# A relative-bias table stored once instead of in 128 copies: a two-layer decoder trunk on one core

## The chip, the cores and the metric

The kernel runs on one core of a Trainium2 chip. The metric is the device time of one execution in microseconds (us). The core has five engines that run side by side and meet through semaphores: TensorE (PE; the profile lists its weight loads apart as PEld), VectorE (DVE), ScalarE (ACT), GpSimd (POOL) and SyncE (SP). Sixteen DMA engines move data between DRAM and the core's memory. A DMA is issued by one of the engines; those of SyncE, ScalarE and GpSimd go through queues of their own to the same sixteen DMA engines.

## The reference, cut to what matters

A sequence of 256 tokens of width 2048 passes two layers, each with a residual, and a last norm. Layer 0 is a gated linear recurrence, layer 1 a sparse attention with three branches (compressed, selected, window) of 16 heads in 4 groups. To the logits of all three branches a relative bias is added, which depends only on the head and on the distance between query and key, through 32 buckets.

```python
def t5_bucket(dist):
    n = jnp.maximum(dist, 0)
...
    return jnp.where(n < max_exact, n, large)
...
    tab = rel_bias.astype(jnp.float32).reshape(NUM_BUCKETS, G, hpg).transpose(1, 0, 2)
...
        logit_c = jnp.einsum('bgqhd,bgkd->bgqhk', qb, K_cmp) + bias_shared(dist_c)
        p_c = masked_softmax(logit_c, (dist_c >= 0)[:, None, :])
...
        logit_s = jnp.einsum('bgqhd,bgqkd->bgqhk', qb, k_g) + bias_s
...
        logit_w = jnp.einsum('bgqhd,bgkd->bgqhk', qb, k_wb) + bias_shared(dist_w)
```

So one table of 16 heads x 256 distances, with a mask value for keys after the query, serves every query: row t of a head's bias is the table, shifted by t.

## The kernel before, in words

**The stream of weights.** All weights are float32 and are read once, in pieces of 128 x 1024 (512 KB). SyncE issues the load of a piece into a `raw` buffer (`emit_load`, L120). ScalarE rounds it to a high part `hi` (L132), VectorE subtracts to get the low part `lo` (L142), and TensorE multiplies in three products: high with high, high with low, low with high (`mm3`, L150). A `plan` lists the pieces in order. Six `raw` buffers and four pairs of split buffers let loads run up to eight pieces and splits up to four pieces ahead of the products; a buffer is loaded again when VectorE has made the low part out of it.

**The other work** is written as generators, which take a step before and a step after the products of each piece (`run`, `advance`). This fixes each engine's order of instructions in the program; the engines then run through their own orders as far as semaphores let them.

**Layer 0** makes four passes (s = 0 to 3), each over four chunks of 512 columns: `f`, `q`, `v`, `z`. Once the `q` chunk is multiplied, VectorE scales it into `QQ` (L439), multiplies by the gate (L457), and TensorE starts the products of the scores (L472), which come behind the first piece of the `v` chunk. Once `v` is multiplied, ScalarE evacuates it (L445).

**The bias table.** `setup` makes it at the start: GpSimd fills `bk` with the bucket number of every distance (L351), by falling distance, VectorE compares to get one-hot columns, one product with the 32 x 16 parameter gives 16 x 256 values, and VectorE copies them into `brev` (L383), 16 rows of 384; the last 128 columns hold the mask value (L352). `store_bias` writes it to DRAM: four DMAs issued by GpSimd (L405), one per four heads, each writing every row 128 times, so that the DRAM tensor `brev_dram` has a copy for each of the 128 partitions. It is started with a delay of eight pieces after layer 0's first `f` chunk, and its steps put four turns between the DMAs.

**The skewed reads.** For each group of four heads in layer 1, `get_bias` issues two DMAs on GpSimd (L836), each for two heads: partition p reads 256 values of its own copy, from column 127 - p. So partition p holds the bias of query p (and of query 128 + p, with other columns), key by key. Group 0's are issued after the window values' projection, those of the next group at the tenth turn of `attend`, when VectorE has done its last head; two buffers.

**Attention.** `attend` runs a head in three slots: TensorE's logits, VectorE's sums with the bias with a running maximum, six per head (`biased`, L871: 128, 7, 128, 256, 15 and 256 keys), ScalarE's exponentials (L878), the weighing by VectorE (L889) and ScalarE (L887), TensorE's transposes (L898). The 7 and the 15 compressed keys read the bias at every 16th column. Slices of the tile `bi` at L860 to L865 pick the columns:

```python
            bi = bias[h // 2][:, h % 2]
...
                   (0, b0[:, 0:7], bi[:, 159:256:16], l[:, 256:263]),
...
                   (4, b1[:, 0:256], bi, l[:, 304:560]),
```

Of the kernel before, what the change touches and what calls it, by code (L numbers as in the profile page):

```python
# [45 lines left out]
def kernel(ctx: ExitStack, tc: tile.TileContext, x, norm_gains, final_gain, rel_bias,  # L46
# [40 lines left out]
        nc.vector.tensor_copy(dst, tp[:, :S])  # L87
        nc.vector.tensor_scalar(scaled, tp[:, :S], QSCALE, None, op0=ALU.mult)

    # ---- the stream of weights: pieces are loaded ahead, split exactly into two parts that one-pass  # L90
    # float32 products carry, and multiplied; between pieces, steps of the other work run ----
    plan = []
    loaded, parts = {}, {}
    steps = []
# [101 lines left out]
            if j == 0 and between:  # L196
                between()

    # Each slot multiplies one piece. A step of other work takes a turn before the products (work that
    # depends on earlier slots) and one after them (products, and what may wait), in turn.  # L200
    def run(gen, delay=0):
        def late():
            for _ in range(2 * delay):
# [62 lines left out]
            advance()  # L266

    x1_dram = dram.tile([S, D], F32, name="x1_dram")
    brev_dram = dram.tile([P, NH, 384], F32, name="brev_dram")

    ctxs = {n: ExitStack() for n in ("xg", "start")}
    xgp = ctxs["xg"].enter_context(tc.tile_pool(name="xgp", bufs=1))
# [17 lines left out]
    pair = lambda ap: ap.rearrange("p (a t) -> p a t", a=2)  # L290
    hgain = pcol[:, 0, 48:49]

# [1 line left out]
    sp = ctxs["start"].enter_context(tc.tile_pool(name="start", bufs=1))  # L294
    xt = sp.tile([P, 2, D], F32, name="xt")
    ssqp = sp.tile([P, 2, 4], F32, name="ssqp")
# [34 lines left out]
        rstd_of(rstd0, ssq, D)  # L331

    prow = sp.tile([P, 2, P], F32, name="prow")
    brev = const.tile([NH, 384], F32, name="brev")
    rb = sp.tile([BUCKETS, NH], F32, name="rb")

    def setup():
        # masks of the levels inside a 32 x 32 block: the highest bit in which t and s differ, s < t
        si = sp.tile([P, 32], I32, name="si")
        ti = sp.tile([P, 32], I32, name="ti")  # L340
        nc.gpsimd.iota(si, pattern=[[0, 32]], base=0, channel_multiplier=1)
        nc.gpsimd.iota(ti, pattern=[[1, 32]], base=0, channel_multiplier=0)
        pidx = sp.tile([P, 1], F32, name="pidx")
        nc.gpsimd.iota(pidx, pattern=[[0, 1]], base=0, channel_multiplier=1, allow_small_or_imprecise_dtypes=True)
        thr = sp.tile([P, 7, 32], F32, name="thr")
        for l in range(7):
            nc.gpsimd.memset(thr[:, l], float(2 ** l // 2))
        bk = sp.tile([BUCKETS, 256], F32, name="bk")
        for b in range(BUCKETS):
            n0, n1 = T5_LO[b], (T5_LO[b + 1] if b + 1 < BUCKETS else 256)  # L350
            nc.gpsimd.memset(bk[:, 256 - n1:256 - n0], float(b))  # L351
        nc.gpsimd.memset(brev[:, 256:], NEG)  # L352
        for _ in range(6):
            yield
        nc.vector.tensor_scalar(si, si, 31, None, op0=ALU.bitwise_and)
        xi = sp.tile([P, 32], I32, name="xi")
        nc.vector.tensor_tensor(xi, si, ti, op=ALU.bitwise_xor)
        nc.vector.tensor_scalar(rowmask, pidx, float(CMP_BLOCK - 1), None, op0=ALU.is_ge)
        oneh = sp.tile([BUCKETS, 256], F32, name="oneh")
        nc.vector.tensor_scalar(oneh, bk, pidx[:BUCKETS], None, op0=ALU.is_equal)  # L360
        gt = sp.tile([P, 32], F32, name="gt")
        nc.vector.tensor_tensor(gt, ti, si, op=ALU.is_ge)
        xf = sp.tile([P, 32], F32, name="xf")
        nc.gpsimd.tensor_copy(xf, xi)
        yield
        yield
        cg = sp.tile([P, 7, 32], F32, name="cg")
        nc.vector.tensor_tensor(cg, xf[:, None, :].to_broadcast([P, 7, 32]), thr, op=ALU.is_ge)
        nc.vector.tensor_mul(cg, cg, gt[:, None, :].to_broadcast([P, 7, 32]))
        mf = sp.tile([P, 6, 32], F32, name="mf")  # L370
        nc.vector.tensor_sub(mf, cg[:, 0:6], cg[:, 1:7])
        nc.gpsimd.tensor_copy(masks, mf)
        yield
        yield
        yield
        pp = aux_bank()
        for i in range(2):
            nc.tensor.transpose(pp[:, i * P:(i + 1) * P], prow[:, i, :], ident)
        nc.tensor.matmul(pp[:NH, 256:512], rb, oneh, start=True, stop=True)
        yield  # L380
        nc.vector.tensor_copy(pcol.rearrange("p a b -> p (a b)"), pp[:, :2 * P])
        # relative bias by reversed distance, masked keys at NEG; one row per partition for skewed reads
        nc.vector.tensor_copy(brev[:, :256], pp[:NH, 256:512])  # L383
        yield
        # lower bounds: softmax over the depth rows, cumulated up to row 0
        lb3 = pcol[:, 0, 0:48].rearrange("p (a h) -> p a h", a=3)
        lbm = sp.tile([P, NH], F32, name="lbm")
        lbe = sp.tile([P, 3, NH], F32, name="lbe")
        nc.vector.tensor_max(lbm, lb3[:, 0], lb3[:, 1])
        nc.vector.tensor_max(lbm, lbm, lb3[:, 2])  # L390
        nc.vector.tensor_sub(lbe, lb3, lbm[:, None, :].to_broadcast([P, 3, NH]))
        yield
        nc.scalar.activation(lbe, lbe, AF.Exp)
        lbs = sp.tile([P, NH], F32, name="lbs")
        yield
        nc.vector.tensor_add(lbs, lbe[:, 0], lbe[:, 1])
        nc.vector.tensor_add(lbs, lbs, lbe[:, 2])
        nc.vector.reciprocal(lbs, lbs)
        nc.vector.tensor_mul(lb, lbe[:, 0], lbs)
        nc.vector.tensor_scalar(oml, lb, -1.0, 1.0, op0=ALU.mult, op1=ALU.add)  # L400

    def store_bias():
        for i in range(4):
            hs = slice(4 * i, 4 * i + 4)
            nc.gpsimd.dma_start(brev_dram[:, hs].rearrange("p h j -> h p j"),  # L405
                                brev[hs, None, :].to_broadcast([4, P, 384]))
            for _ in range(4):
                yield

# [1 line left out]
    HG = {}  # L411

    def f_of(s, ps):
# [182 lines left out]
        add_chunk(w_in1, 4096 + 512 * s, 512, "n", X, v_done)  # L596
        add_chunk(w_in1, 6144 + 512 * s, 512, "n", X, on_z)

# [1 line left out]
    ssq1 = const.tile([P, 2, 4], F32, name="ssq1")  # L600
    ssum = const.tile([P, 2], F32, name="ssum")
    tok = lambda ap, c0, n: ap[:, c0:c0 + n].rearrange("(t p) c -> p t c", p=P)
# [59 lines left out]
        add_chunk(w_out1, 512 * c, 512, "n", (yh, yl), on_x1(c),  # L662
                  extra={1: [residual(("x", c - 1), x_rows, 512 * (c - 1), 512)]} if c else None)

# [1 line left out]
    NS = {}  # L666

    def open_ns():
# [14 lines left out]
        NS["hid"], NS["gelu"] = (scratch[:, c0:c0 + 64].rearrange("p (g n) -> p g n", g=G) for c0 in (512, 576))  # L683
        NS["bia"] = scratch[:, 640:641]
        nc.gpsimd.memset(NS["hid"][:, :, NCMP:], 0.0)
        # three products of the two parts in one: high, low and high parts below each other
        for name, shape in (("Vc", [P, 512]), ("pc", [P, 2, 2, P])):
            NS[name] = n1.tile(shape, F32R, name=name)
            nc.gpsimd.memset(NS[name].bitcast(F32), 0.0)
# [142 lines left out]

    def get_bias(g, a):
        b = NS["p2"].tile([P, 2, S], F32, tag="bias", name="bias", bufs=BIAS_BUFS)
        src = brev_dram[:, 4 * g + 2 * a:4 * g + 2 * a + 2, :]
        nc.gpsimd.dma_start(b, bass.AP(tensor=src.tensor, offset=src.offset + HD - 1,  # L836
                                       ap=[[NH * 384 - 1, P], [384, 2], [1, S]]))
        NS["bias"][a] = b

    def attend(g):  # L840
# [3 lines left out]
        pT, L = {}, {}  # L844

        def logits(h):
            # keys of a group: the first compressed 8 again, selected 256, compressed 16, window 256
            b0, b1, b2 = aux_bank(), aux_bank(), aux_bank()
            ks = [t[:, g] for t in NS["K"]]
            first = [bass.AP(tensor=k.tensor, offset=k.offset, ap=[list(k.ap[0]), [280, 2], [1, 136]]) for k in ks]  # L850
            for tt, dst, (kh, kl) in ((0, b0[:, 0:272], first), (1, b1[:, 0:272], [k[:, 8:280] for k in ks]),
                                      (1, b2[:, 0:256], [k[:, 280:536] for k in ks])):
                qh, ql = (t[:, h % 2, tt * P:(tt + 1) * P] for t in NS["q", g, h // 2])
                mm3(dst, qh, ql, kh, kl, True, True)
            l = ns.tile([P, 816], F32, tag="L", name="L", bufs=1)
            mx = ns.tile([P, 6], F32, tag="mx", name="mx")
            sm = ns.tile([P, 6], F32, tag="sm", name="sm")
            bi = bias[h // 2][:, h % 2]
            nc.gpsimd.memset(l[:, 263:288], 0.0)
            prt = ((1, b0[:, 8:136], bi[:, 128:256], l[:, 0:128]),  # L860
                   (0, b0[:, 0:7], bi[:, 159:256:16], l[:, 256:263]),
                   (2, b0[:, 136:264], bi[:, 128:256], l[:, 128:256]),
                   (4, b1[:, 0:256], bi, l[:, 304:560]),
                   (3, b1[:, 256:271], bi[:, 31:256:16], l[:, 288:303]),
                   (5, b2[:, 0:256], bi, l[:, 560:816]))  # L865
            L[h] = l, sm, prt, mx
# [104 lines left out]
    def gated(g, ps, ov):  # L971
# [6 lines left out]
        for a in range(2):  # L978
            nc.scalar.activation(zs[a], zs[a], AF.Silu)
        if g + 1 < G:  # L980
            # the exponential's table is loaded back ahead of its use
            nc.scalar.activation(NS["one"], NS["one"], AF.Exp, scale=0.0)
        steps_between = (3, 2, 5) if g + 1 < G else (1, 2, 2)
        for _ in range(steps_between[0]):
# [39 lines left out]
        else:  # L1024
            add_chunk(w_in2, C_Z + 512 * g, 512, "t", X, z_done1(g))

# [1 line left out]
    FN = {}  # L1028

    def open_fin():  # L1030
# [113 lines left out]
```

## Time and profile before

| What | Value |
|---|---|
| Median of three runs | 1010.38 us (1009.32 to 1012.52) |
| Span of the profiled execution | 1007.5 us |
| Mean granted clock of TensorE | 0.990 |
| DMA packets, bytes | 105405, 182.28 MB |
| Read from DRAM, written to DRAM | 173.62 MB, 7.34 MB |

The profiled execution's span, from its first to its last instruction, is 1007.5 us; the runs' times hold a little more than a span, and the median stands 2.9 us above it. In the profile a row of the page's slices is the span cut into 40 pieces of 25.2 us, each digit the busy share in tenths. A group row has the line, the engine, the operation, what is written from what, a count, and then busy time and the mean length of one. A row of waits names who waited for whom, the total, how often, and the longest. DMA rows give the size of one transfer and the median time from its issue to its landing.

### The profile page before, as it was taken

The page shows a single profiled execution, that of the slowest core. Times are in us where ns is not written, and L with a number is a line of the kernel's source. Part 1 is how long each engine was busy: PE and PEld are TensorE (multiplying, and loading weights), DVE is VectorE, ACT ScalarE, POOL GpSimd, SP SyncE. Part 2 cuts the span into 40 slices and gives each one's busy share as a digit, 9 for nine tenths or more (in the row PEclk, how much of TensorE's full clock was granted, in tenths as well). Part 3 has the DMA queues.
Part 4 walks back from the last instruction along what each step waited for, and adds up shares of the span by engine and source line. Part 5 has one row for each costly group of instructions (what it writes and reads, how often), then busy time and mean ns, then how long its engine had stood idle before and what let it go on. Part 6 is the DMA issues. An engine that isn't in the chain of part 4 may idle for free.

```text
span 1007.5 us, 19899 instructions
## 1 busy us (share of the span) xinstructions
PE 979.9 (97%) x8001; PEld 906.5 (90%) x8001; DVE 630.1 (63%) x1194; ACT 519.4 (52%) x896; POOL 55.0 (5%) x157
## 2 busy tenths in 40 slices
PE   8949999999999999999999999999999999999997
PEld 7947899789978997888889999899999999998887
DVE  6718555855586558655556565555677787776564
ACT  6603455245524552454444554443766877875442
POOL 2200100010001000100002000000000000000000
PEclk9978999999999999999999999999999999999999
DMA  9797656465646454647677776566454545456662
GB/s 325 151 137 221 197 154 189 130 198 153 188 129 202 151 189 128 202 158 234 218 233 237 226 217 190 154 208 189 147 148 131 166 137 155 129 166 230 208 215 99
DMA packets 105405, 182.28 MB, mean 181 GB/s; under 512 B 8128, under 2 KB 27152, under 8 KB 105184
## 3 DMA queue, kind: packets, MB, share of 16 engines
q1 hardware_dynamic: 100512, 171.86, 54.4%
q0 software_dynamic: 4464, 8.61, 4.7%
q8 instruction: 63, 1.03, 0.4%
q10 hardware_dynamic: 336, 0.54, 0.1%
q14 instruction: 30, 0.25, 0.1%
HBM read 173.62 MB, written 7.34 MB: 180 GB/s over the span
## 4 chain that ended last, share of the span: by engine, by line
PE 93%; DMA 4%; ACT 1%; DVE 1%; issue 1%; SPq 0%; POOLq 0%; POOL 0%; DVEq 0%; ACTq 0%
PE mainps L150 82%; PE auxps L150 5%; DMA raw<-in_hgrn_w_in_dram 3%; PE auxps L472 2%; DMA xt<-in_x_dram 1%; PE auxps L898 1%; PE auxps L483 0%; PE auxps L531 0%; PE auxps L529 0%; PE auxps L530 0%; PE auxps L487 0%; PE auxps L554 0%; PE auxps L629 0%; PE auxps L900 0%; ACT hi L132 0%
## 5 line engine op out<-in xcount | busy, mean ns | idle before, releaser
L142 DVE TENSOR_TENSOR lo<-raw,hi 128x1024 fp32r<-128x1024 f32 (+3 forms) x317 | 380.6, 1208 | 198.1 <-ACT hi L132 197.2
L132 ACT CAST hi<-raw 128x1024 fp32r<-128x1024 f32 (+3 forms) x317 | 328.5, 1038 | 340.8 <-PE mainps L150 293.9
L150 PE MATMUL mainps<-xh,hi 128*128 128x256 f32 x1280 | 365.4, 286 | 0.0
L150 PE MATMUL mainps<-xh,lo 128*128 128x256 f32 x1280 | 362.1, 283 | 0.0
L150 PE MATMUL mainps<-xl,hi 128*128 128x256 f32 x1280 | 362.0, 283 | 0.0
L150 PEld LDWEIGHTS mainps<-xh,hi 128*128 128x128 f32 x1280 | 244.8, 191 | 0.8 <-ACT hi L132 0.4
L150 PEld LDWEIGHTS mainps<-xl,hi 128*128 128x128 f32 x1280 | 244.9, 191 | 0.2
L150 PEld LDWEIGHTS mainps<-xh,lo 128*128 128x128 f32 x1280 | 244.7, 191 | 0.0
L150 PE MATMUL mainps<-hi,xh 128*128 128x512 f32 (+1 forms) x352 | 135.1, 384 | 0.0
L150 PE MATMUL mainps<-lo,xh 128*128 128x512 f32 (+1 forms) x352 | 131.5, 374 | 0.0
L150 PE MATMUL mainps<-hi,xl 128*128 128x512 f32 (+1 forms) x352 | 131.2, 373 | 0.0
L150 PE MATMUL mainps<-hi,yh 128*128 128x512 f32 (+1 forms) x288 | 105.9, 368 | 0.0
L150 PE MATMUL mainps<-hi,yl 128*128 128x512 f32 (+1 forms) x288 | 105.3, 366 | 0.0
L150 PE MATMUL mainps<-lo,yh 128*128 128x512 f32 (+1 forms) x288 | 105.3, 366 | 0.0
L150 PEld LDWEIGHTS mainps<-hi,xl 128*128 128x128 f32 x352 | 66.5, 189 | 11.7
L150 PEld LDWEIGHTS mainps<-hi,xh 128*128 128x128 f32 x352 | 66.5, 189 | 11.7 <-issue 0.2
L150 PEld LDWEIGHTS mainps<-lo,xh 128*128 128x128 f32 x352 | 66.6, 189 | 10.2
L150 PEld LDWEIGHTS mainps<-hi,yl 128*128 128x128 f32 x288 | 54.3, 189 | 8.8
L150 PEld LDWEIGHTS mainps<-hi,yh 128*128 128x128 f32 x288 | 54.4, 189 | 8.5
L150 PEld LDWEIGHTS mainps<-lo,yh 128*128 128x128 f32 x288 | 54.4, 189 | 8.5
L878 ACT ACTIVATE L<-L,mx 128x128 f32<-128x128 f32 (+1 forms) x96 | 37.6, 393 | 24.3 <-DVE mx L873 24.2
L472 PEld LDWEIGHTS auxps<-QQ,Kg 128*32 128x32 f32 x1280 | 15.0, 113 | 21.7 <-DVE QQ L457 14.9
(241 smaller groups left out, 868.9 us busy)
## 6 DMA issues: line engine op xcount, KB each, us to landing
raw<-in_hgrn_w_in_dram SPq DMA_DIRECT2D x127, 512.0 KB, 3.7
raw<-in_nsa_w_in_dram SPq DMA_DIRECT2D x104, 512.0 KB, 3.9
raw<-in_hgrn_w_out_dram SPq DMA_DIRECT2D x32, 512.0 KB, 5.0
raw<-in_nsa_w_out_dram SPq DMA_DIRECT2D x32, 512.0 KB, 4.4
raw<-in_nsa_w_in_dram SPq DMA_DIRECT2D x10, 420.0 KB, 3.3
brev_dram<-brev POOLq DMA_DIRECT2D x4, 768.0 KB, 37.7
xt<-in_x_dram SPq DMA_DIRECT2D x8, 256.0 KB, 8.2
raw<-in_x_dram SPq DMA_DIRECT2D x4, 512.0 KB, 4.3
```

Of the source, the lines that this page charges most:

```text
L132: nc.scalar.copy(hi[:, :m], raw[:, :m])
L142: nc.vector.tensor_sub(lo[:, :m], raw[:, :m], hi[:, :m].bitcast(F32))
L150: nc.tensor.matmul(dst, a, b, start=first and n == 0, stop=last and n == 2, skip_group_check=True)
L472: nc.tensor.matmul(dst[32 * b:32 * b + 32, i0 % 4:(i1 - 1) % 4 + 1, j, :], Kg[:, cs], QQ[:, q0:2, cs], start=True, stop=True, tile_positio ...
L878: nc.scalar.activation(dst, dst, AF.Exp, bias=mx[:, i:i + 1], accum_out=sm[:, i:i + 1])
L898: nc.tensor.transpose(t1[:, i * P:(i + 1) * P], l[:, c0:c0 + P], ident)
```

## The change

The table is kept by rising distance, in a row `brow` of 384 columns: column 127 + n holds distance n, and every other column holds the mask value. `store_bias` writes its 16 rows once to DRAM, `bias_dram`, with a single DMA on GpSimd (L403 of the changed kernel). In `get_bias`, partition p reads 256 values from column p on, all partitions from the same table, so that the tile holds the bias with the keys reversed. `logits` turns the view round: `bi` starts at the last column and steps by -1, so that the six sums read the same values for the same keys, at a step of -1 (and -16 for the compressed keys). GpSimd's memset of the table covers 384 columns instead of 128. On all engines the order of the instructions stays as it is, apart from the four stores that become one.

```diff
-    brev_dram = dram.tile([P, NH, 384], F32, name="brev_dram")
+    bias_dram = dram.tile([NH, 384], F32, name="bias_dram")
...
-            nc.gpsimd.memset(bk[:, 256 - n1:256 - n0], float(b))
-        nc.gpsimd.memset(brev[:, 256:], NEG)
+            nc.gpsimd.memset(bk[:, n0:n1], float(b))
+        nc.gpsimd.memset(brow, NEG)
...
-        nc.vector.tensor_copy(brev[:, :256], pp[:NH, 256:512])
+        nc.vector.tensor_copy(brow[:, HD - 1:HD - 1 + 256], pp[:NH, 256:512])
...
     def store_bias():
-        for i in range(4):
-            hs = slice(4 * i, 4 * i + 4)
-            nc.gpsimd.dma_start(brev_dram[:, hs].rearrange("p h j -> h p j"),
-                                brev[hs, None, :].to_broadcast([4, P, 384]))
-            for _ in range(4):
-                yield
+        nc.gpsimd.dma_start(bias_dram, brow)
+        yield
...
-        src = brev_dram[:, 4 * g + 2 * a:4 * g + 2 * a + 2, :]
-        nc.gpsimd.dma_start(b, bass.AP(tensor=src.tensor, offset=src.offset + HD - 1,
-                                       ap=[[NH * 384 - 1, P], [384, 2], [1, S]]))
+        src = bias_dram[4 * g + 2 * a:4 * g + 2 * a + 2, :]
+        nc.gpsimd.dma_start(b, bass.AP(tensor=src.tensor, offset=src.offset, ap=[[1, P], [384, 2], [1, S]]))
...
             bi = bias[h // 2][:, h % 2]
+            bi = bass.AP(tensor=bi.tensor, offset=bi.offset + S - 1, ap=[list(bi.ap[0]), [-1, S]])
```

More of the change, by code (lines that the diff above doesn't have):

```diff
@@ L333 @@
     prow = sp.tile([P, 2, P], F32, name="prow")
-    brev = const.tile([NH, 384], F32, name="brev")
+    brow = const.tile([NH, 384], F32, name="brow")
     rb = sp.tile([BUCKETS, NH], F32, name="rb")
```

## The prediction

> **What bounds the kernel now.** I began with the profile page: engine shares, and the slices.
>
> ```profile
> PE 979.9 (97%) x8001; PEld 906.5 (90%) x8001; DVE 630.1 (63%) x1194; ACT 519.4 (52%) x896; POOL 55.0 (5%) x157
> PE   8949999999999999999999999999999999999997
> PEclk9978999999999999999999999999999999999999
> brev_dram<-brev POOLq DMA_DIRECT2D x4, 768.0 KB, 37.7
> ```
>
> TensorE (PE) works in every slice but one: the third, 50 to 75 us, shows 4 tenths, and its granted clock dips there. So this is a PE-bound kernel with one hole. Work taken off other engines, or bytes taken off the DMA engines, are worth nothing outside that hole unless PE waits for them. The fourth line makes a suspect: the four stores of the bias table, 768 KB each, which take 37.7 us to land.
>
> Next come the waits of PE alone (who waited for whom, total, times, longest), and then the chain of waits from 59 to 130 us.
>
> ```profile
> PE auxps L472 <- DVE QQ L457: 14.5, 1, 14.5
> ```
>
> ```profile
> 42.55 29.97 DMA raw<-in_hgrn_w_in_dram
> ...
> 72.62 1.05 ACT hi L132
> 73.67 0.02 issue
> 73.69 1.23 DVE lo L142
> 74.92 1.20 DVE QQ L439 x2
> 76.12 0.61 DVE QQ L457
> 76.72 0.04 issue
> 76.77 1.93 PE auxps L472 x64
> ```
>
> PE waits once for long: 14.5 us, for VectorE (DVE) at L457. The chain says that DVE was not the cause. DVE works in order, its `QQ` products stand behind the split of a weight piece (L142), that split behind ScalarE's (L132), and that behind a load of a piece which took 29.97 us. The third view says what that load stood behind: the DMA queues between 42 and 62 us (packets, MB, share of 16 engines), then the issues (KB each, us to landing).
>
> ```profile
> q0 software_dynamic: 967, 1.93, 89.5%
> q1 hardware_dynamic: 126, 0.25, 3.2%
> ...
> raw<-in_hgrn_w_in_dram SPq DMA_DIRECT2D x5, 512.0 KB, 30.0
> brev_dram<-brev POOLq DMA_DIRECT2D x1, 768.0 KB, 42.0
> ```
>
> Queue q0 carries what GpSimd (POOL) issues, here only the bias stores; q1 carries SyncE's weights. The stores hold 89.5% of the engines' time and the weights get 3.2%. When do the stores start, and how long do the prefetched pieces last? POOL's and PE's rows in the timeline:
>
> ```profile
> 38.45 4.46 POOL L405 DMA_DIRECT2D brev_dram<-brev  x4
> ```
>
> ```profile
> 61.91 0.39 PE L150 MATMUL mainps<-hi,xl 128*128 128x512 f32 x1
> 76.77 1.93 PE L472 MATMUL auxps<-QQ,Kg 128*32 128x64 f32 x64 [14.47 <-DVE QQ L457]
> ```
>
> All four stores are issued together at 38.45, though the code spreads them by turns: the turns place them in POOL's stream, and nothing in it between them waits. PE runs on for 23.9 us from pieces already loaded, then stops at 62.3.
>
> **What the stores cost.** I compare the same work with and without them: from the first product of the `v` chunk to the first evacuation of that chunk (ScalarE L445), in pass 0 and pass 1 of layer 0's loop. The window view gives busy time and instructions for PE, PEld, DVE, ACT, POOL, then clock, DMA share, GB/s.
>
> ```profile
> 59.38:104.82 45.44, 30.97 (x464) 24.25 (x463) 27.65 (x65) 11.42 (x15) 3.63 (x8) 0.81 0.80 187
> 177.54:205.86 28.32, 28.32 (x464) 22.25 (x463) 26.25 (x64) 9.32 (x13) 3.64 (x8) 1.00 0.42 126
> ```
>
> Both hold 464 matmuls. Without stores the work takes 28.32 us, with them 45.44: 17.12 us more. Two terms make that up:
>
> ```profile
> 62.31:76.77 14.46, 0.00 (x1) 0.00 (x1) 3.08 (x5) 1.04 (x1) 0.00 (x0) 0.59 1.00 158
> 76.77:82.33 5.56, 5.56 (x73) 4.64 (x74) 2.36 (x4) 1.83 (x2) 0.00 (x0) 0.53 0.95 292
> ```
>
> PE stands still for 14.46 us and then runs 5.56 us at a granted clock of 0.53, which loses 5.56 x 0.47 = 2.6. Together 17.1, as by the pairs. That the clock costs more than the idle time alone is also in the Trainium skill, TensorE: Matmul & The Clock Gate, Part 1: an idle window of about 3.4 us halves the clock, and about 3.4 us of work brings it back. By that rule the cold term would be an estimated 1.7 and the sum 16.2; here the cold stretch lasted 5.56 us, and the measurement decides.
>
> **The change, part by part.**
>
> *Store.* Four stores (3072 KB together) become one of 16 rows x 384 floats, 24 KB. The same size occurs among POOL's loads:
>
> ```profile
> prow<-in_hgrn_lb_dram POOLq DMA_DIRECT2D x1, 24.0 KB, 4.5
> ```
>
> So its landing lies between 4.5 us and, if a store behaves like the old ones whatever its size, 37.7; by bytes it is 1/128 of the old 42 us of hogging, 0.3 us. I take the small end: weights have 23.9 us of cover and need more than a landing to be starved, they need the engines held. The table's first reader comes after the whole of layer 0 and layer 1's keys and values. What is late next in the freed stretch? In pass 1 nothing: PE is busy for all of 28.32 us at a DMA share of 0.42. Gain: 17.1.
>
> *Table.* GpSimd fills 16x384 instead of 16x128 with the mask value, some 0.2 us more, and afterwards idles:
>
> ```profile
> POOL xf L364 <- DVE rowmask L358: 11.4, 1, 11.4
> ```
>
> The 11.4 us hide it. The bucket fills and the DVE copy keep their sizes and only change columns. Nothing.
>
> *Skewed reads.* Still 128 partitions x 2 heads x 1 KB per read, eight reads. What is new is that all 128 partitions read overlapping parts of the same 3 KB of DRAM. POOL's issue of a later group's read, DVE's first use of it, and the landing of such reads:
>
> ```profile
> 740.74 0.71 POOL L836 DMA_DIRECT2D bias<-brev_dram  x1 [0.33 <-issue]
> ```
>
> ```profile
> 754.91 0.29 DVE L871 CUSTOM_DVE_ANT_0 L<-auxps,bias 128x128 f32<-128x128 f32 x1 [0.44 <-issue]
> ```
>
> ```profile
> bias<-brev_dram POOLq DMA_DIRECT2D x8, 256.0 KB, 3.4
> ```
>
> 14.2 us lie between issue and use, 3.4 are needed: 10.8 spare. No trace shows reads from one spot; bounds are no change and a landing past 14.2. I take no change, the nearest row being the same transfer.
>
> *Reversed operand.* DVE's 96 bias additions (L871) read the bias with step -1 or -16 instead of 1 or 16. Grouped by shape (count, busy us, mean ns), with a product that reads both inputs at step 2 (L500, 128x256):
>
> ```profile
> L871 DVE CUSTOM_DVE_ANT_0 L<-auxps,bias 128x256 f32<-128x256 f32 x32 | 13.4, 419 | 0.0
> L871 DVE CUSTOM_DVE_ANT_0 L<-auxps,bias 128x128 f32<-128x128 f32 x32 | 9.2, 289 | 5.5 <-PE auxps L150 3.9 <-issue 1.2
> L500 DVE TENSOR_TENSOR TT<-Fg 128x256 f32<-128x256 f32 x8 | 3.4, 419 | 0.0
> L871 DVE CUSTOM_DVE_ANT_0 L<-auxps,bias 128x15 f32<-128x15 f32 x16 | 2.7, 170 | 0.0
> L871 DVE CUSTOM_DVE_ANT_0 L<-auxps,bias 128x7 f32<-128x7 f32 x16 | 2.6, 160 | 0.0
> ```
>
> At step 1 an element costs (419 - 289)/128 = 1.02 ns; at step 16 (170 - 160)/8 = 1.25 ns; a step of 2 on both inputs costs nothing. No row has a negative step; bounds are 0 and a doubled element, 790 elements x 1.02 = 0.8 us per head. I take 0: the direction matters less than a distance that already costs next to nothing. What hides it is thin, see below.
>
> Sum: span 1007.5 - 17.1 = 990.4. The span lies 2.9 under the median of 1010.38; with the same around it, 993.3.
>
> **Rivals.**
>
> *The reversed read is slow (0.07).* DVE's weighing of a head (L889) and PE's transposes of it (L898), two heads:
>
> ```profile
> 771.92 0.76 DVE L889 TENSOR_SCALAR L<-L,sm 128x128 f32<-128x128 f32 x4
> 783.62 0.76 DVE L889 TENSOR_SCALAR L<-L,sm 128x128 f32<-128x128 f32 x4
> ```
>
> ```profile
> 773.13 0.60 PE L898 MATMUL auxps<-ident,L 128*128 128x128 f32 x4
> ```
>
> ```profile
> 786.00 0.60 PE L898 MATMUL auxps<-ident,L 128*128 128x128 f32 x4
> ```
>
> From L889's end to the transposes 0.45 us are spare on the second and fourth heads of a group, 1.6 on the others. A doubled element delays L889 by 0.8, so 8 heads stall 0.35 each: 3 us, at most 16 x 0.8 = 13. Time 996.3, at most 1006.4.
>
> *Weights are late anyway (0.04).* If the early loads can't keep up without stores either, half the hole stays: 1010.4 - 8.6 = 1001.8. Against it: the share of 0.42 in pass 1, and the 9 tenths of PE's second slice.
>
> *The hole has another cause (0.02).* Then 1010.4. Against it stand 89.5% and 3.2%.
>
> *One hot spot in DRAM: slower (0.03).* All 128 partitions' reads meet in 3 KB. If a read then holds the engines as the stores did, weights starve as then. The reads go out in pairs, four in all, and PE has 23.9 us of cover; a pair must hold the engines longer than 23.9 us before it costs, and over 28.2 (14.1 us a read) before four of them eat the 17.1 gained. If a pair held them as long as the four stores' 42 us: 4 x 18 = 72 us, and 1010.4 - 17.1 + 72 = 1065. Against it: 4.1 times the present 3.4 us are needed. For it the Trainium skill, DMA: Bandwidth & Descriptors, Latency and other measured facts: rows at large power-of-two pitches fell to half rate, which it ascribes, unverified, to channel aliasing. Half rate here is an estimated 6.8 us a read, still hidden; no run here shows it.
>
> **How the numbers follow.** The forecast, 0.84, is 993.3. The runs shown spread from -1.1 to +2.1 around their median; the cold stretch may differ by a microsecond. So 991 at the low end; at the high end the slow read's 996.3 with the same spread, 998. Left out are the worst of that case and the last three, about 0.12. A measurement of this kernel tells about 0.3%, 3 us, from no change. Faster: 0.84 + 0.07 + 0.04 = 0.95; same 0.02; slower 0.03.
>
> **What would show it.** In the changed kernel's trace: no wait of PE for L457's successor above 1 us; weight loads between 42 and 62 us landing in about 4 us; no dip of the granted clock in the third and fourth slices; the `v` stretch of pass 0 taking 28 to 29 us like pass 1's; the store landing under 5 us and the reads at 3 to 7; the 128x256 addition at 419 ns. I am wrong if the hole remains, if the addition goes above 600 ns with PE waiting at the transposes, or if reads land after 14 us.

## The result, and the profile after

The changed kernel takes 992.64 us in the median of four runs (992.32 to 993.57), the kernel before 1010.73 (1009.32 to 1012.52). The ratio is 0.9827, with a 95% interval of 0.9814 to 0.9841. The forecast was 993.3. The ratios below are each to runs of the kernel before made in the same round as the run, with medians of 1008.97 to 1009.93 us.

The page of the changed kernel, the lines that answer to those shown of before:

```profile
span 991.7 us, 19895 instructions
PE 978.8 (99%) x8001; PEld 906.0 (91%) x8001; DVE 630.3 (64%) x1194; ACT 519.1 (52%) x896; POOL 51.2 (5%) x154
PE   8999999999999999999999999999999999999997
PEclk9999999999999999999999999999999999999999
```

PE's busy time is the same to about 1 us (979.9 before), the span is 15.8 us shorter, and the third slice, with its dip of PE and of the clock, reads 9 in both. All of the gain is idle and slow time. All the waits of PE, then the DMA queues and issues between 42 and 62 us, and last the issue of the new store, which leaves at 39 us:

```profile
PE auxps L1101 <- DMA gn<-in_norm_gains_dram: 3.8, 1, 3.8
PE auxps L312 <- DMA xt<-in_x_dram: 0.9, 1, 0.9
PE auxps L895 <- DVE L L886: 0.6, 1, 0.6
```

```profile
q1 hardware_dynamic: 1904, 3.67, 60.7%
...
raw<-in_hgrn_w_in_dram SPq DMA_DIRECT2D x7, 512.0 KB, 3.7
```

```profile
bias_dram<-brow POOLq DMA_DIRECT2D x1, 24.0 KB, 1.8
```

The wait of 14.5 us is gone and no other took its place. In the same 20 us the weights' queue moves 3.67 MB where it moved 0.25, GpSimd's queue moves nothing, a piece lands in 3.7 us where it took 30.0, and the new store lands in 1.8. The stretch by which the prediction priced the hole, the `v` chunk of pass 0, in the window view:

```profile
60.11:88.58 28.47, 28.47 (x464) 22.26 (x463) 26.24 (x64) 9.31 (x12) 3.61 (x8) 1.00 0.44 124
```

The same 464 matmuls take 28.47 us, where they took 45.44: 16.97 less, against 17.12 forecast. The bias additions by shape, and the landings of the bias reads (first of the kernel before, then of this one):

```profile
L868 DVE CUSTOM_DVE_ANT_0 L<-auxps,bias 128x256 f32<-128x256 f32 x32 | 13.4, 419 | 0.0
...
L868 DVE CUSTOM_DVE_ANT_0 L<-auxps,bias 128x15 f32<-128x15 f32 x16 | 2.7, 171 | 0.0
```

```profile
DMA to landing us min/median/max: 3.1/3.4/4.3
```

```profile
DMA to landing us min/median/max: 3.5/4.3/4.8
```

A negative step costs nothing that shows. The reads from one spot are 0.9 us slower in the median; a later group's are still used 14.2 us after their issue (724.95 and 739.12 us), and nothing waits for them.

### The profile page after: what moved, and what is told of

Same layout as the page of the kernel before. It is cut to its first block, busy times and chain, and to the rows that moved or that the text cites. A ratio compares the mean times of both kernels' runs of the same rounds, so it can differ in the third digit from the quotient of the medians.

```text
span 991.7 us, 19895 instructions
## 1 busy us (share of the span) xinstructions
PE 978.8 (99%) x8001; PEld 906.0 (91%) x8001; DVE 630.3 (64%) x1194; ACT 519.1 (52%) x896; POOL 51.2 (5%) x154
## 4 chain that ended last, share of the span: by engine, by line
PE 97%; ACT 1%; DMA 1%; issue 1%; DVE 0%; SPq 0%; POOLq 0%; POOL 0%; DVEq 0%
PE mainps L150 86%; PE auxps L150 5%; PE auxps L468 2%; PE auxps L895 1%; DMA xt<-in_x_dram 1%; PE auxps L479 0%; PE auxps L312 0%; PE auxps L527 0%; PE auxps L526 0%; PE auxps L525 0%; PE auxps L483 0%; PE auxps L625 0%; PE auxps L550 0%; PE auxps L897 0%; PE auxps L474 0%
## 5 line engine op out<-in xcount | busy, mean ns | idle before, releaser
L875 ACT ACTIVATE L<-L,mx 128x128 f32<-128x128 f32 (+1 forms) x96 | 37.5, 392 | 24.3 <-DVE mx L870 24.2
L913 DVE TENSOR_TENSOR pl<-auxps,ph 128x512 fp32r<-128x512 f32 (+1 forms) x32 | 17.5, 556 | 16.3 <-ACT ph L909 14.7
```

The source lines that it names most:

```text
L875: nc.scalar.activation(dst, dst, AF.Exp, bias=mx[:, i:i + 1], accum_out=sm[:, i:i + 1])
L913: nc.vector.tensor_sub(pl[:, ks, hh, :], t, ph[:, ks, hh, :].bitcast(F32))
```

## The experiments

The changes agree with the forecast; the question left was why 3 MB of stores made a hole of 17 us. My theory had been that the stores hold the DMA engines for 42 us together, 10.5 each, and that only what goes beyond PE's 23.9 us of loaded pieces costs. The rival: the cost goes with the bytes. In all the kernels below that add stores to the changed kernel, the DRAM tensor they write is read by nobody.

**The four stores back: e1_copies_back.** The diff against the changed kernel:

```diff
+        for i in range(4):
+            hs = slice(4 * i, 4 * i + 4)
+            nc.gpsimd.dma_start(copies_dram[:, hs].rearrange("p h j -> h p j"),
+                                brow[hs, None, :].to_broadcast([4, P, 384]))
```

> The changed kernel, and the four old stores of 768 KB as well, into a DRAM tensor that nobody reads. Theory (the gain is PE's hole behind the stores, nothing else): the hole is back, 1009 to 1011 us, PE waiting 14 to 15 us for L457's successor and a granted clock of about 0.5 behind it. Rival (the gain came from the reads or from the reversed operand, or from fewer steps in the program): it stays at 992 to 994.

Measured: 1009.6 us (1009.16 to 1011.13), a ratio to the kernel before of 1.0005 (0.9995 to 1.0014). PE's longest wait:

```profile
PE auxps L473 <- DVE QQ L458: 14.1, 1, 14.1
```

The stores alone bring the whole time back, with the new reads and the reversed operand in place. That they are the cause is shown.

**The reversed operand alone: e2_copies_reversed.** The changed kernel with 128 copies stored as before, by rising distance, and each partition reading its own:

```diff
-        nc.gpsimd.dma_start(bias_dram, brow)
+        for i in range(4):
+            hs = slice(4 * i, 4 * i + 4)
+            nc.gpsimd.dma_start(bias_dram[:, hs].rearrange("p h j -> h p j"),
+                                brow[hs, None, :].to_broadcast([4, P, 384]))
...
+                                       ap=[[NH * 384 + 1, P], [384, 2], [1, S]]))
```

> The reversed operand alone: 128 copies are stored and read as before, but by rising distance, and VectorE reads with step -1. Theory (a negative step costs nothing): 1009 to 1011, the 128x256 addition at 419 ns, no new wait of PE at the transposes. Rival (it costs a part that the gain hides): 1011.5 or more, additions above 430 ns.

Measured: 1009.12 us, ratio 1.0 (0.9991 to 1.0009); the 128x256 addition at 418 ns. **And without it: e8_forward**, where the line that turns the view round is left out:

> The changed kernel without the reversed view: VectorE reads the bias at step 1, so the bias is that of other keys and the output another. Theory (the negative step costs nothing): 992 to 993.5, as the changed kernel. Rival: it is 1 us or more below the changed kernel.

Measured: 991.9 us (991.65 to 993.58), ratio 0.9825 (0.9811 to 0.984), and the changed kernel's was 0.9827 (0.9814 to 0.9841); the addition at 419 ns. From both sides the negative step is free within 0.2% of the time. The runs alone could not exclude the rival's 1 us, which lies within their spread; the additions, of the same length to 1 ns, do.

**The stores spread: e3_spread.** In the kernel before, each store is placed behind GpSimd's copies of another pass:

```diff
+    def store_bias(i):
+        hs = slice(4 * i, 4 * i + 4)
+        nc.gpsimd.dma_start(brev_dram[:, hs].rearrange("p h j -> h p j"),
+                            brev[hs, None, :].to_broadcast([4, P, 384]))
...
+        if a == 0:
+            store_bias(s)
```

> The kernel before with its 128 copies, but each of the four stores is placed in GpSimd's stream behind its work of another pass of layer 0, so that they leave some 100 us apart. Theory (only what goes beyond PE's 23.9 us of loaded pieces costs): each store holds the engines 10.5 us, a quarter of 42, PE never waits: 992 to 994, with all 3 MB still written. Rival (cost goes with the bytes written): 1009 to 1011. Between: four small holes of 1 to 2 us each, 997 to 1001.

Measured: 1050.25 us (1049.93 to 1051.6), ratio 1.0405 (1.039 to 1.0421). The theory fell, and so did both other numbers. PE's longest waits, and the queues and issues around the first store, 90 to 118 us:

```profile
PE mainps L150 <- ACT hi L132: 45.8, 4, 12.8
```

```profile
q1 hardware_dynamic: 1296, 2.50, 30.3%
q0 software_dynamic: 537, 0.72, 24.2%
...
raw<-in_hgrn_w_in_dram SPq DMA_DIRECT2D x5, 512.0 KB, 26.7
```

A single store of 768 KB makes the weights land after 26.7 us although it takes 24.2% of the engines and the weights only 30.3%: nearly half of the sixteen engines' time is idle in a stretch in which PE waits for weights. A quarter of the engines is four of sixteen, and a store has four rows. Against the changed kernel's 992.64 the four spread stores cost 57.6 us, 14.4 each. So a store isn't a quarter of the hole; each makes one, and the old code had paid for one by sending all four at once.

**How many stores: e9_one_store, e5_two_stores, e6_eight_stores.** As e1, with `range(1)`, `range(2)` and eight stores (the last four into a second set of copies). The expectations for two and for eight are those of the old theory:

> The changed kernel, and two of the old four stores as well (1.5 MB), into an unread DRAM tensor. Theory (a hold of the engines is free up to PE's 23.9 us of loaded pieces): two stores hold them 21 us, no wait or one under 2 us: 992 to 995. Rival (cost in proportion to bytes, 17.1 us for four): 1001.

> The changed kernel, and eight old stores as well (6 MB). Theory (past the cover each further store costs what it holds the engines, 10.5 us, less what weights trickle through): 1010 + 42 less up to a half: 1030 to 1052. Rival (in proportion to bytes): 992.6 + 34 = 1027.

That for one is by the new theory:

> The changed kernel, and only one of the old four stores as well (768 KB, four rows), into an unread DRAM tensor. Theory, formed after the spread stores: each old store runs on four of the sixteen DMA engines for some 33 us, whatever runs beside it; a piece of weights needs all sixteen and is as late as its slowest part, so one store makes nearly the hole of four: 1005 to 1010, q0 at about a quarter of the engines' share. Rival (in proportion to bytes): 997.

| Old stores | Median us (range) | Ratio to before (95%) |
|---|---|---|
| none | 992.64 (992.32 to 993.57) | 0.9827 (0.9814 to 0.9841) |
| 1 | 1008.28 (1007.35 to 1009.49) | 0.9985 (0.9975 to 0.9994) |
| 2 | 1008.81 (1007.66 to 1009.91) | 0.9991 (0.9982 to 1.0001) |
| 4 | 1009.6 (1009.16 to 1011.13) | 1.0005 (0.9995 to 1.0014) |
| 8 | 1024.65 (1022.33 to 1030.91) | 1.0156 (1.0122 to 1.019) |

The queues between 42 and 62 us, with one old store and then with two:

```profile
q1 hardware_dynamic: 1008, 1.96, 33.6%
q0 software_dynamic: 241, 0.51, 24.3%
...
raw<-in_hgrn_w_in_dram SPq DMA_DIRECT2D x6, 512.0 KB, 26.2
```

```profile
q0 software_dynamic: 1093, 0.99, 48.1%
q1 hardware_dynamic: 557, 1.08, 17.9%
...
raw<-in_hgrn_w_in_dram SPq DMA_DIRECT2D x5, 512.0 KB, 29.2
```

One store came out as its theory had it; two missed both of their numbers. The shares are 24.3, 48.1 and 88.4 (in e1) for one, two and four: each store takes four engines of its own. The Trainium skill, DMA: Bandwidth & Descriptors, "Why a DMA increments its semaphore by 16 and not by 1", states this rule: the slowest dimension sets how many engines a DMA runs on, four rows give four, and stores from GpSimd take their engines in turn. The shares agree, and in the trace with one store never more than four of its data packets are under way at once. Landing times agree with engines side by side: 33.6 us for one store, 37.9 in the median for four. A weight piece is spread over all sixteen engines: in the changed kernel's view of 42 to 62 us, where only weights move, slices of half a us show the sixteen busy at 90% or more. It is complete when its last part is, so it matters that some engines are held, hardly how many; this last step is argued from the table, and no run follows the parts of one piece. Eight stores put a second set behind the first on the same engines (their share stays at 88.4%): PE waits 14.6 and then 10.4 us, and the time is 15 us more than with four. That is under both expectations, and how the 15 come about wasn't followed further.

**Why a store is slow.** One store moves 0.51 MB in 24.3% of 16 x 20 us = 77.8 us of engine time: 6.6 GB/s an engine, 26 for the four (the trace's records of these transfers show packets of 4608 B that take 693 ns). Four explanations were told apart: the way the copies lie in DRAM, the source's rows, GpSimd's queue as such, and the number of rows. First the source, with 128 partitions read once each, **e4_wide_source**:

```diff
+        xs = xh.rearrange("p k t -> p (k t)").bitcast(F32).rearrange("p (b w) -> p b w", w=512)
+        for i in range(4):
+            nc.gpsimd.dma_start(copies_dram[:, 4 * i:4 * i + 4],
+                                xs[:, i:i + 4, :384])
```

> The changed kernel, and four stores of 768 KB as well, issued where the old ones were, into an unread DRAM tensor, in rows of 384 floats as before; but each reads 128 partitions once, not 4 partitions 128 times. Theory (the old stores were slow because all their reads met in 4 partitions): they land like the stores of x1, 512 KB in 6.2 us, the four in 12 to 15 us, PE does not wait: 992 to 994. Rival (3 MB written from GpSimd's queue hold the engines whatever the source): four landings of 33 to 42 us, 1009 to 1011.

Measured: 992.65 us (991.56 to 993.68), ratio 0.9836 (0.9819 to 0.9852).

```profile
copies_dram<-xh POOLq DMA_DIRECT2D x4, 768.0 KB, 6.8
```

The same bytes, from the same queue and at the same place in the program, are free. Next, 16 rows in each store, so that each runs on sixteen engines, **e7_sixteen_rows**:

```diff
+        for i in range(4):
+            nc.gpsimd.dma_start(copies_dram[32 * i:32 * i + 32].rearrange("p h j -> h p j"),
+                                brow[:, None, :].to_broadcast([NH, 32, 384]))
```

> The changed kernel, and the same 3 MB of copies as well, issued in the same place, but each of the four stores writes 32 copies of all 16 rows, so that it reads 16 partitions 32 times instead of 4 partitions 128 times. Theory (reads that meet in few partitions set the pace): with four times the partitions the stores are up to four times as fast, all within 12 to 20 us: 992 to 995. Rival (few-partition reads don't matter, the broadcast or GpSimd's queue does): 1009 to 1011.

Measured: 1006.68 us (1005.81 to 1009.59), ratio 0.997 (0.9959 to 0.9982).

```profile
q0 software_dynamic: 481, 1.99, 93.6%
...
raw<-in_hgrn_w_in_dram SPq DMA_DIRECT2D x5, 512.0 KB, 27.7
```

A miss for the theory, and 2 us below the rival's range: 1.99 MB in 93.6% of 320 us is 6.6 GB/s an engine again. The four old stores together had read the same 16 rows already; only their order changed, and the engines that each one store uses.

E4 had changed the layout in DRAM too, so both sides were tried apart: 128 source partitions at the old addresses, **e10_pitch_wide**, and the old source with the copies of a row one behind the other, **e11_contiguous_copies**:

```diff
+        xs = xh.rearrange("p k t -> p (k t)").bitcast(F32)
+        for i in range(NH):
+            nc.gpsimd.dma_start(copies_dram[:, i], xs[:, 128 * i:128 * i + 384])
```

```diff
+    copies_dram = dram.tile([NH, P, 384], F32, name="copies_dram")
...
+        for i in range(4):
+            hs = slice(4 * i, 4 * i + 4)
+            nc.gpsimd.dma_start(copies_dram[hs], brow[hs, None, :].to_broadcast([4, P, 384]))
```

> The changed kernel, and 3 MB as well into an unread DRAM tensor, at the old stores' addresses in DRAM (rows of 1536 B, 24 KB apart one after the other), but in sixteen stores of 192 KB that read 128 partitions once each. If the source sets the pace (one engine reads one partition again and again): these are fast, each landing within 8 us, 992 to 994. If the pitch in DRAM does: they land as slowly as the old ones, together 30 us and more, 1005 to 1011.

> The changed kernel, and four stores of 768 KB as well that read four partitions 128 times each, as the old ones, but write their 128 copies of a row one behind the other in DRAM, not 24 KB apart. If the source sets the pace: as slow as the old ones, landings of 33 to 42 us, 1008 to 1011. If the pitch in DRAM does: landings of 7 to 15 us, 992 to 995.

Measured: 992.7 us, ratio 0.9827 (0.9812 to 0.9843), and 1010.66 us, ratio 1.0008 (0.9999 to 1.0018). The issues of the one and of the other:

```profile
copies_dram<-xh POOLq DMA_DIRECT2D x16, 192.0 KB, 5.5
```

```profile
copies_dram<-brow POOLq DMA_DIRECT2D x4, 768.0 KB, 37.8
```

The layout in DRAM is out; the source sets the pace. What about it: one engine reading one partition 128 times, or four engines reading four neighbours? **e12_spread_partitions** keeps four rows read 128 times each and puts them four partitions apart:

```diff
+        xs = xh.rearrange("p k t -> p (k t)").bitcast(F32)
+        for i in range(4):
+            p0 = 64 * (i // 2) + 16 * (i % 2)
+            nc.gpsimd.dma_start(copies_dram[:, 4 * i:4 * i + 4].rearrange("p h j -> h p j"),
+                                xs[p0:p0 + 16:4, None, :384].to_broadcast([4, P, 384]))
```

> The changed kernel, and four stores of 768 KB as well, to the old addresses, each reading four partitions 128 times, as the old ones; but the four lie four apart (0, 4, 8, 12 and so on; rows of another tile, into an unread DRAM tensor). In all slow stores so far the four engines that worked side by side read four neighbouring partitions, and got 4 x 4608 B in 693 ns, 26.6 GB/s together. If neighbouring partitions share one way out (the Trainium skill, SBUF - State Buffer, gives partitions 0 to 3 one port): landings of 8 to 15 us, 992 to 994. If reading one partition again and again is slow by itself: 33 to 42 us, 1008 to 1011.

Measured: 992.5 us (991.55 to 993.89), ratio 0.9834 (0.9816 to 0.9852). Its queues and issues between 42 and 62 us, then the median landing of all four stores:

```profile
q0 software_dynamic: 2685, 3.16, 51.0%
q1 hardware_dynamic: 1555, 3.01, 42.5%
...
raw<-in_hgrn_w_in_dram SPq DMA_DIRECT2D x7, 512.0 KB, 11.3
copies_dram<-xh POOLq DMA_DIRECT2D x3, 768.0 KB, 19.8
```

```profile
copies_dram<-xh POOLq DMA_DIRECT2D x4, 768.0 KB, 18.1
```

3.16 MB in 51.0% of 320 us is 19.4 GB/s an engine, three times as much, from rows read as often. Reading one partition repeatedly isn't slow; four engines on four neighbouring partitions are, with 26 GB/s between them. One rival is left by the edits alone: every slow store read the table's tile, every fast one another tile, `xh`. The trace of e3 answers it. At the start of two of its stores, one engine reads its row of the table for a moment with no other data packet of the store under way (to within 5 ns); these three packets of 4608 B take 200, 189 and 176 ns, as in e12 (180 in the median), against 693 with four engines at work. So the table's tile is not slow in itself, as far as three packets tell. The expected 8 to 15 us of landing were missed (18.1; weights now share the engines' time about evenly, 42.5%), the time was met. The Trainium skill, SBUF — State Buffer, "Door 1: The DMA port swizzle", gives partitions 0 to 3 one of sixteen ports, and all ports together 435 GB/s, an estimated 27.2 each: the measured 26 agrees. Only two groupings were tried, neighbours and four apart; that the map holds elsewhere isn't shown here, and neither are neighbouring partitions of another tile.

## Why the prediction was right, point by point

- **The hole behind the stores.** Right, and shown by e1. The price by equal work was 17.12 us; the same stretch now shows 16.97, and in the runs the medians differ by 1010.73 - 992.64 = 18.1, against the forecast's 17.1 and within the spread of the four runs of before. With the kernel before at the 1009.4 to 1009.9 us of the later rounds on which e1 to e11 rest, the difference would be about 17.
- **The 2.9 us around the span.** Mis-sized, and it came out near by luck. A run's time lies 1.8 us above its own span in each run that has both on record (993.57 and 991.7, for one). So the span of before, 1007.5, belongs to a run of 1009.3, the fastest of its four, and the other 1.1 of the 2.9 were the choice of that run. The profiled run of the changed kernel is the slowest of its four; its span is 991.7, while the four spans' middle is 990.9. The forecast was thus 1.1 too high in this term and 0.5 too low in the span, and the one partly cancelled the other.
- **The span.** 990.4 was expected, 991.7 came in the profiled run. Pass 0's `v` chunk starts at 60.11 instead of 59.38, 0.73 later, and up to there PE waited for no store in either kernel. Nearly all of it, 0.70, is there at PE's first product with a weight piece, which starts at 9.12 instead of 8.42 us. In the traces of the experiments this start lies anywhere between 7.67 (e6) and 9.39 us (e2), long before the first store of the table leaves, so this term is spread of the start and not the change. Another 0.45 goes in layer 0's later passes. The last evacuation of the `z` chunk, before and after, lies 15.79 us apart:

```profile
430.93 1.27 ACT L451 ACTIVATE sz<-mainps,rstd 128x512 f32<-128x512 f32 x2
```

```profile
415.14 1.27 ACT L447 ACTIVATE sz<-mainps,rstd 128x512 f32<-128x512 f32 x2
```

  So 16.97 - 0.73 - 0.45 = 15.8, the whole difference of the spans. The 0.45 was not traced to a cause.
- **The new store.** "Between 4.5 us and 37.7" was wrong as a bound: it landed in 1.8. A load of the same size was too far a row for the lower end. It made no difference.
- **The table and the reversed operand.** Right: no wait of PE at the transposes beyond the 0.6 us of before, additions at 419 ns, e2 and e8.
- **The skewed reads.** Taken as unchanged, they went from 3.4 to 4.3 us, far from the 14 us at which it would have cost. In all runs reads from the one table landed after 4.0 to 4.6 us in the median, reads from copies after 3.4 to 3.9. With e2's 3.9 and 4.0 in three kernels with the one table, that it is the shared spot which costs isn't shown.
- **The cover.** Here the reasoning was right about the case and wrong as a rule. The prediction let PE's 23.9 us of loaded pieces stand against the time for which the engines are held, all of them, and priced a tiny store "by bytes" at 1/128 of 42 us. The spread stores show that holding a quarter of the engines is enough, and one store of 768 KB costs 15.6 us (1008.28 - 992.64), nearly all of what four cost. By bytes it would have been 4. By these runs what counts is for how long any engine is held: 33 us with one store, against the 23.9 of cover, while in e12, where the slowest store landed after 21.1, PE did not wait. The hot-spot rival's threshold, a pair of reads that holds the engines for 23.9 us, rests on the right quantity only if "the engines" means any of them.

## What to carry to other kernels

When a prefetched stream starves beside a small transfer, look at that transfer's landing time and its number of rows rather than at its bytes or at the mean share of the DMA engines: a DMA that keeps four of sixteen engines busy for 33 us holds up every load that is spread over sixteen (26.2 us to landing here, against 3.7). Don't let a broadcast store read a few neighbouring partitions many times over; put the rows four apart, spread the source over all partitions, or store once and let the reads do the copying. And to price a hole in the trace, time the same instructions in a pass that has none: idle time alone, 14.5 us, missed the 2.6 that the slow clock behind it took.

## What the runs showed of the hardware that I had not expected

- Four DMA engines that read four neighbouring partitions get 6.6 GB/s each, 26 together; four apart, 19.4 each beside the weights. A packet of 4608 B takes 693 ns in the one case, 180 in the other.
- Spreading a harmful transfer over time made it more than three times as harmful: four stores some 115 us apart cost 57.6 us over the changed kernel, the same four at once 17.0.
- A DVE addition with a maximum reads its second input at step -1 as fast as at step 1 (419 ns for 128x256), and at -16 as at 16 (171 and 170 ns for 128x15).
- 128 partitions that read overlapping parts of one 3 KB table land a little later than from copies of their own (medians of 4.0 to 4.6 and of 3.4 to 3.9 us for 256 KB); the cause isn't shown.
